# Three pairs of w_conv_out's columns as seven products each, with gate, shift and operand sums on GpSimd

## The chip, the core and the metric

The kernel runs on one core of a Trainium2 chip. It is measured in device microseconds, start to end of one execution. Five engines work from queues of their own: TensorE (PE; its weight loads are listed as PEld), VectorE (DVE), ScalarE (ACT), GpSimd (POOL) and SyncE (SP), which here issues nearly all DMAs. An instruction waits on semaphores for what it needs, and behind it waits everything in its engine's queue.

## The reference, cut to what matters

One layer of a transformer trunk: 128 context tokens and 512 latent ones (640 columns in all), width 1024, float32.

```
ada = silu(c) @ w_ada + b_ada              # six parts: sh1, sc1, g1, sh2, sc2, g2
u   = rms_norm(h) * (1 + sc1) + sh1
z   = u @ w_in                             # q, k, v, b_gate, c_gate, x_in, g_att, g_conv
att  = attention(q, k, v) @ w_att_out
conv = (b_gate * dwconv3(c_gate * x_in)) @ w_conv_out
m   = sigmoid(g_att) * att + sigmoid(g_conv) * conv
h   = h + g1 * rms_norm(m @ w_o)
u   = rms_norm(h) * (1 + sc2) + sh2
h   = h + g2 * rms_norm((silu(g) * val) @ w_down),   [g, val] = dwconv3(u @ w_up)
```

The change lies between the gates and `m`: it touches how `conv`, the gate `g1` and the second half of the shift `sh2` are computed.

## The kernel before, in words

Every float32 product is made of three matmuls: weights and right operand are cut into a high part (ACT rounds it) and a low part (VectorE subtracts), and `mm3` adds high x high, high x low and low x high. The 640 tokens are two halves of 320 (`HT`). A weight tile is 128 x 1024: eight blocks of 128 rows for one tile of 128 output columns (`col_load`, `raw_tile`, three buffers), with `hi_of` (line 1173, ACT) and `lo_of` (line 1177, VectorE) for the parts.

*Plain columns.* `plain_gemm` makes one tile of output columns: 8 blocks x 3 matmuls x 2 halves = 48 matmuls of 320 columns.

*Pairs.* `mix(m, extra)` makes two tiles of output columns from seven products where 2 x 2 quarters would take eight: the weights of the two tiles give A11, A12, A22 and four sums S1 to S4 (`msums`, line 1281, four additions of 128 x 512), the right operand gives B11, B21, B22 and the sums T1 to T4. One product is `block`: 4 blocks x 3 matmuls = 12. The seven follow as A11, A12, S2, S1, S3, S4, A22, with ACT's and VectorE's work written between them; S2 and S1 use the weight sums s1, s2 (part 1), S3 and S4 use s3, s4 (part 2), S2 uses T2, S1 T1, S3 T3, A22 T4, S4 B22. Three PSUM banks take the products; ACT copies one (`copied`) and VectorE adds the other (`added`, line 1197). `extra` holds work of other kinds by slot: slot 0 is ahead of A11, slot 1 ahead of A12, 2 ahead of S2, 3 ahead of S1, 4 ahead of S3, 5 ahead of S4, 6 ahead of A22.

*The order of the stages around the change.* After attention and the eight columns of `w_att_out` come 19 pairs of `w_in`: three of g_att (GA), then four times C, X and B, which give `c_gate`, `x_in` and `b_gate` for two tiles each, then four of g_conv (GC). With every C, X, B the convolution's taps (`conv_tap`, line 1405) and products run on VectorE, and its result is stored as `BH`, `BL`, the high and low part (`b_hi`, `b_lo`), the right operand of `w_conv_out`. Then come the eight columns of `w_conv_out`, all by `plain_gemm`, each followed on VectorE by the product with sigmoid(g_conv), the sum with `MA` (the attention's part, line 1525), and the two parts `MH`, `ML` for `w_o`. Then `w_o`: first columns 0 to 511 in four quarters of two blocks, for five tiles of tokens, then columns 512 to 1023.

*Gates.* The gates are products of two vectors (silu of c and of c_ctx) with `w_ada`. `gate_add` (line 292) multiplies a 128-row block of `w_ada` by one number per partition and adds it to a sum, on VectorE; `gate_sums` (line 301) adds over the partitions with four matmuls against ones. Before, the second half of `sh2` (columns 512 to 1023, 512 columns wide) runs on VectorE in the pairs 0 to 7, with `gate_sums` ahead of pair 9 and the way through DRAM (`sht`) to columns by pair 12. The whole of `g1` (1024 wide) runs on VectorE in the eight columns of `w_conv_out`, sixteen passes, with `gate_sums` and `gate_rows` in the second quarter of `w_o`; its rows go through DRAM (`bct`) to `WR` in the third quarter.

*What sets the order.* The orders of TensorE, ACT and VectorE are those in which the program writes them (`fixed`). GpSimd's and SP's instructions are put in order by a planner with costs of its own, except in blocks under `manual_schedule` for that engine; the eight columns of `w_conv_out` are such a block for SP. Rooms in SBUF are named (`r0` to `r7b`); a new tile in a room waits for the last use of the old one.

Of the kernel before, what the change touches and what calls it, by code (L numbers as in the profile page):

```python
# [11 lines left out]
F32 = mybir.dt.float32  # L12
F32R = mybir.dt.float32r
# [4 lines left out]
D = 1024  # L18
# [45 lines left out]
def trunk_layer(ctx, tc, x_prompt, x_sample, cache_k, cache_v, c, c_ctx, w_ada, b_ada, g_pre1, g_post1, g_pre2,  # L64
# [209 lines left out]

    def gate_load(raw, kind, k, c0=0):
        nc.sync.dma_start(raw, w_ada[k * 128:(k + 1) * 128, kind * D + c0:(kind + 1) * D])

# [976 lines left out]
    PAIRS = [("GA", i) for i in range(1, 4)] + [(x, i) for i in range(4) for x in "CXB"] + [("GC", i) for i in range(4)]  # L1254
    NP = len(PAIRS)
    AT = {"GA": O_GA, "C": O_C, "X": O_X, "B": O_B, "GC": O_GC}
    ROWS_OF = {"C": 0, "X": 1, "B": 2}

    def mrows(m):
        x, i = PAIRS[m]  # L1260
        r = ROWS_OF[x] if x in ROWS_OF else (i - 1 if x == "GA" else i)
        return ROWS[2 * r], ROWS[2 * r + 1]

    def col_load(key, w, c0):
        raw = raws[key] = raw_tile()
        nc.sync.dma_start(raw.rearrange("p (k c) -> p k c", c=128), w[:, c0:c0 + 128].rearrange("(k p) c -> p k c", p=128))

    def mload(n):

        if n < 2 * NP:  # L1270
            x, i = PAIRS[n // 2]
            col_load(("m", n // 2, n % 2), w_in, AT[x] + (2 * i + n % 2) * 128)
        elif n < 2 * NP + KT:
            col_load(("v", n - 2 * NP), w_conv_out, (n - 2 * NP) * 128)

    def msums(m):
        a1, a2 = raws["m", m, 0], raws["m", m, 1]
        s1, s2, s3, s4 = (MS[:, i * 512:(i + 1) * 512] for i in range(4))

        def add(out, a, b):  # L1280
            V.tensor_tensor(out=out, in0=a, in1=b, op=ALU.add)  # L1281

        def both():
            add(s1, a2[:, 0:512], a2[:, 512:1024])
            add(s3, a1[:, 0:512], a2[:, 0:512])
        return both, lambda: add(s2, s1, a1[:, 0:512]), lambda: add(s4, s2, a1[:, 512:1024])

    def mhi(m, part):
        src = {0: raws["m", m, 0], 1: MS[:, 0:1024], 2: MS[:, 1024:2048], 3: raws["m", m, 1][:, 512:1024]}[part]
        hi_of(("m", m, part), src)  # L1290
# [5 lines left out]
    def mix(m, extra):  # L1296

        d0, d1 = mrows(m)
        nxt = m + 1 if m + 1 < NP else None
        pair["m", m] = tuple(bank((3 * m + i) % 8)[:, 0:HT] for i in range(3))  # L1300

        def step(x):
            b = 1 if x == "A12" else 2 if x in ("S1", "S4") else 0
            part, half = PLACE[x]
            block(pair["m", m][b], ("m", m, part), half, "m" + RIGHT[x], x in ("A11", "A12", "S1"), True)

# [3 lines left out]

        if m:
            mix_last(m - 1)
# [27 lines left out]
        lo_of(("m", m, 3))  # L1340
        mload(2 * m + 4)
        if nxt:
            mhi(nxt, 0)
            lo_of(("m", nxt, 0))
            adds[1]()
        else:
            vcut(0)
# [6 lines left out]
        if nxt:  # L1354
            adds[2]()
        mload(2 * m + 5)
        more(6)
# [61 lines left out]
    SHIFTS = {(0, 4): ((0, 0), (0, 1)), (1, 1): ((1, 0), (1, 1)), (2, 1): ((2, 0), (2, 1)), (3, 1): ((3, 0), (3, 1)), (4, 1): ((4, 0), (4, 1)),  # L1419
              (4, 4): ((5, 0), (5, 1)), (7, 1): ((6, 0),), (7, 4): ((6, 1), (7, 0), (7, 1))}  # L1420

    def shift_rows():
        p = bank(7)[:, 0:256]
        gate_sums(p, xaccs)
        out = XG[:, 2, 0:256]
        S.activation(out, p, AF.Copy)
        for h in range(2):
            for row in range(2):
                j, r0 = 64 * h + 32 * row, 4 * row + 2 * h
                nc.sync.dma_start(sht[r0:r0 + 2, :].rearrange("(o f) c -> o (f c)", o=1), out[j:j + 1, :])  # L1430
        shr = sm_.tile([KT, 128], F32, name="shr", bufs=1)
        nc.sync.dma_start(shr, sht)
        return shr

# [5 lines left out]

    for k in range(3):
        gate_load(XG[:, 2 + k, :], 3, k, 512)
    for m, (x, i) in enumerate(PAIRS):
        ex = {}
        if m == 9:
            shr = shift_rows()
        elif m == 12:
            shift_columns(shr, bank(7))

# [21 lines left out]
        elif before[0] == "B":  # L1471
# [7 lines left out]
            also(3, b_lo, o, y1)  # L1479
        for slot in (1, 4):  # L1480
            for k, row in SHIFTS.get((m, slot), ()):
                also(slot, gate_add, xaccs, XG[:, 2 + k % 3, :], k, row)
                if row and k + 3 < KT:
                    also(slot, gate_load, XG[:, 2 + k % 3, :], 3, k + 3, 512)
        mix(m, ex)


    MH = [region(rb, f"r5{x}", [4, NTOK], F32R, f"MH{x}") for x in "ab"]
    ML = [region(rb, f"r6{x}", [4, NTOK], F32R, f"ML{x}") for x in "ab"]
    units += [(w_o, 2 * q, 2, 0, 512) for q in range(4)]  # L1490
# [4 lines left out]

    GA0, GA1 = (region(ra, f"r{i}", [5, D], F32, f"GA{i}") for i in range(2))
    gaccs, gvec = [[GA0[:, i, :]] for i in range(2)], GA0[:, 4, :].rearrange("p (i c) -> p i c", i=2)
    graws = [GA1[:, k, :] for k in range(5)] + [GA0[:, k, :] for k in (2, 3)] + [GA1[:, 0, :]]


    loads = ctx.enter_context(ExitStack())
    loads.enter_context(tc.manual_schedule(engines={mybir.EngineType.SP}))
    for j in range(KT):
        if j + 1 < KT:
            vcut(j + 1)
        else:
# [12 lines left out]
        outs = plain_gemm(j + 2, hi, lo, BH, BL)
        sg = ROWS[j]  # L1520
        for h, (out, (b0, b1)) in enumerate(zip(outs, BLKS)):
            times(sg[:, b0:b1], out, sg[:, b0:b1])
            if h == 0 and j:
                gate_add(gaccs, graws[j], j, 0)
        V.tensor_tensor(out=sg, in0=sg, in1=MA[:, j, :], op=ALU.add)
        for row in range(0 if j == 0 else 1, 2):
            gate_add(gaccs, graws[j], j, row)
        mh, ml = MH[j // 4][:, j % 4, :], ML[j // 4][:, j % 4, :]
        S.activation(mh, sg, AF.Copy)
        minus(ml, sg, mh.bitcast(F32))  # L1530

# [388 lines left out]
    for q in range(4):  # L1920
# [7 lines left out]
        elif q == 1:  # L1928
            half_load(0)
            p = bank(6)  # L1930
            gate_sums(p, gaccs)
            gate_rows(p, gvec, GA0[:, 3, 0:512], 0)
            half_cut(0)
# [331 lines left out]
```

## Time and profile before

| | |
|---|---|
| median of 3 runs | 1111.45 us (1111.35 to 1111.68) |
| the profiled execution | 1111.6 us |
| its span, first to last instruction | 1109.7 us |
| granted TensorE clock, mean | 0.999 |
| the 19 pairs of w_in, from the first product | 321.5 to 555.6 us |
| the eight columns of w_conv_out | 555.6 to about 611.9 us |
| GpSimd busy in these two stretches | 0.0 us |

A row of a group gives the line, engine, operation, output <- inputs by the program's names, shapes and count, then after the bar the summed time in us and the mean in ns, then the idle time ahead of these instructions and what ended it. Rows of the timeline have the start and the length in us. The tile `MT` stands for T1 to T4, `UH`, `UL` for the parts of u, `whi`, `wlo` for the parts of a weight tile, `WA`, `WB` for the rows of results and the weight sums, `b` for a PSUM bank of this stage; `s` for one in the attention stage.

### The profile page before, as it was taken

What the parts mean: (1) busy time and instruction counts of PE and PEld (TensorE: products, weight loads), DVE (VectorE), ACT (ScalarE), POOL (GpSimd) and SP (SyncE); (2) the same over time, 40 slices, a digit from 0 to 9 for tenths busy, and PEclk for the clock granted to TensorE, in tenths of its full rate; (3) what the DMA queues carried; (4) which work ended last, traced back from release to release, by engine and by line L of the source; (5) the groups of instructions that cost most, each with busy time, mean ns of one, the idle gap of its engine ahead of it and who ended that gap; (6) DMA issues with size and microseconds to landing.
All of it is one profiled execution on the core that took longest, in us unless ns stands there. A gap on an engine that the chain in (4) does not pass through costs nothing.

```text
span 1109.7 us, 19293 instructions
## 1 busy us (share of the span) xinstructions
PE 1100.2 (99%) x7665; PEld 1014.8 (91%) x7665; DVE 840.1 (76%) x1351; ACT 577.3 (52%) x1021; POOL 146.2 (13%) x190
## 2 busy tenths in 40 slices
PE   8999999999999999999999999999999999999997
PEld 6798888889999999999999789999999999998886
DVE  5687766765548899888678558898899989989544
ACT  5486776664335544455422356655565555546442
POOL 1066566651000000000000022000000000000001
PEclk9999999999999999999999999999999999999999
DMA  9833112102224322332264644234344333435722
GB/s 321 241 100 99 58 40 77 39 2 77 66 89 118 109 76 78 98 93 76 80 207 151 212 170 152 76 100 125 113 130 134 106 114 119 127 100 186 260 91 95
DMA packets 160527, 130.59 MB, mean 118 GB/s; under 512 B 6454, under 2 KB 139054, under 8 KB 160438
## 3 DMA queue, kind: packets, MB, share of 16 engines
q1 hardware_dynamic: 160326, 129.34, 37.4%
q8 instruction: 60, 0.98, 0.4%
q14 instruction: 29, 0.24, 0.1%
q10 hardware_dynamic: 112, 0.04, 0.0%
HBM read 117.91 MB, written 11.44 MB: 117 GB/s over the span
## 4 chain that ended last, share of the span: by engine, by line
PE 96%; DMA 2%; ACT 1%; DVE 1%; POOL 0%; issue 0%; DVEq 0%; SPq 0%; ACTq 0%; POOLq 0%
PE b L1186 45%; PE b L183 10%; PE b L185 9%; PE b L184 9%; PE s L704 3%; PE s L892 3%; PE s L183 3%; PE s L916 3%; PE s L185 3%; PE s L184 3%; DMA raw<-in_w_in_dram 1%; DMA araw<-in_w_ada_dram 1%; PE b L1784 1%; PE s L675 0%; PE s L238 0%; PE b L1634 0%
## 5 line engine op out<-in xcount | busy, mean ns | idle before, releaser
L1186 PE MATMUL b<-ZBr,whi 128*128 128x320 f32 x688 | 152.1, 309 | 0.0
L1186 PE MATMUL b<-MT,whi 128*128 128x320 f32 x608 | 134.2, 309 | 0.0
L1186 PEld LDWEIGHTS b<-ZBr,whi 128*128 128x128 f32 x688 | 114.9, 188 | 0.1
L1186 PE MATMUL b<-ZBr,wlo 128*128 128x320 f32 x344 | 106.1, 308 | 0.0
L1186 PEld LDWEIGHTS b<-MT,whi 128*128 128x128 f32 x608 | 101.6, 188 | 0.0
L1186 PE MATMUL b<-MT,wlo 128*128 128x320 f32 x304 | 94.0, 309 | 0.0
L879 POOL TENSOR_TENSOR pr<-pr,sm 128x640 f32<-128x640 f32 x64 | 80.0, 1260 | 54.6 <-DVE sm L878 48.3
L1173 ACT ACTIVATE whi<-SUM 128x1024 fp32r<-128x1024 f32 x40 | 42.2, 1054 | 78.5 <-DVE SUM L1699 76.0
L1729 DVE SCALAR_TENSOR_TENSOR Y<-C,cffn,Y 128x642 f32<-128x642 f32 x88 | 77.6, 881 | 0.9
L149 DVE TENSOR_TENSOR wlo<-raw,whi 128x1024 fp32r<-128x1024 f32 (+1 forms) x32 | 35.4, 1106 | 53.7 <-ACT whi L148 53.4
L869 ACT ACTIVATE pr<-s,mx,rq 128x640 f32<-128x640 f32 x64 | 56.6, 885 | 32.5 <-DVE mx L856 29.1
L1186 PE MATMUL b<-ZBT,whi 128*128 128x320 f32 x320 | 71.1, 309 | 0.0
L1186 PE MATMUL b<-UL,whi 128*128 128x320 f32 x228 | 70.8, 311 | 0.0
L1186 PE MATMUL b<-UH,wlo 128*128 128x320 f32 x228 | 70.0, 307 | 0.0
L1186 PE MATMUL b<-UH,whi 128*128 128x320 f32 x228 | 69.7, 306 | 0.0
L1173 ACT ACTIVATE whi<-WB 128x1024 fp32r<-128x1024 f32 x38 | 40.1, 1055 | 54.9 <-DVE WB L1281 54.9
L1177 DVE TENSOR_TENSOR wlo<-raw,whi 128x1024 fp32r<-128x1024 f32 (+1 forms) x51 | 50.4, 1018 | 21.7 <-ACT whi L1173 21.6
L1186 PEld LDWEIGHTS b<-ZBr,wlo 128*128 128x128 f32 x344 | 64.6, 188 | 0.0
L183 PE MATMUL s<-whi,UH 128*128 128x256 f32 (+1 forms) x197 | 64.4, 327 | 0.0
L1194 ACT ACTIVATE p<-b 128x320 f32<-128x320 f32 x78 | 34.2, 438 | 56.7 <-PE b L1186 54.8
L851 DVE TENSOR_REDUCE mx<-s 128x1 f32<-128x640 f32 x64 | 52.5, 820 | 14.6 <-PE s L704 14.2
L185 PE MATMUL s<-whi,UL 128*128 128x256 f32 (+1 forms) x197 | 59.8, 304 | 0.0
(401 smaller groups left out, 3191.5 us busy)
## 6 DMA issues: line engine op xcount, KB each, us to landing
raw<-in_w_in_dram SPq DMA_DIRECT2D x48, 512.0 KB, 3.8
RAW<-in_w_up_dram SPq DMA_DIRECT2D x40, 512.0 KB, 5.0
raw<-in_w_down_dram SPq DMA_DIRECT2D x22, 512.0 KB, 5.0
raw<-in_w_ada_dram SPq DMA_DIRECT2D x18, 512.0 KB, 5.1
actd<-Y SPq DMA_DIRECT2D x18, 321.0 KB
XT<-in_w_ada_dram SPq DMA_DIRECT2D x9, 512.0 KB, 9.7
raw<-in_w_conv_out_dram SPq DMA_DIRECT2D x9, 512.0 KB, 3.8
raw<-in_w_att_out_dram SPq DMA_DIRECT2D x8, 512.0 KB, 3.9
```

What stands on the lines that cost most here:

```text
L149: V.tensor_tensor(out=lo[:, :n], in0=raw, in1=hi[:, :n].bitcast(F32), op=ALU.subtract)
L183: PE.matmul(out, ah, bh, start=start, stop=False)
L184: PE.matmul(out, ah, bl, start=False, stop=False)
L185: PE.matmul(out, al, bh, start=False, stop=stop)
L851: V.tensor_reduce(out=mx, in_=self.sc[h], axis=AX.X, op=ALU.max, negate=True)
L869: S.activation(pr, self.sc[h], AF.Exp, bias=mx, scale=rs, accum_out=sm)
L879: G.tensor_tensor(out=pr, in0=pr, in1=sm.broadcast_to((128, NTOK)), op=ALU.mult)
L1173: S.activation(to[0], raw, AF.Copy)
L1177: V.tensor_tensor(out=lo, in0=raw, in1=hi.bitcast(F32), op=ALU.subtract)
L1186: PE.matmul(out, p[:, ws], q[:, k, :], start=start and k == 0 and n == 0, stop=stop and k == 3 and n == 2, skip_group_check=True)
L1194: S.activation(t, pair[j][b], AF.Copy)
L1729: V.scalar_tensor_tensor(out=y, in0=crows(j)[i][:, d:d + NACT], scalar=cffn[:, 44 * d + o:44 * d + o + 1], in1=y, op0=ALU.mult, op1=ALU.add)
```

## The change

- **w_conv_out.** Columns 0 and 1 stay plain. Columns 2 to 7 become three pairs (`PAIRS += [("O", 1..3)]`, `mix` with m = 19, 20, 21). Their right operands are quarters of `BH`, `BL` and four sums oT1 to oT4, kept in the room of u's parts. oT1 (B12 - B11) is built during the w_in pairs: the difference on GpSimd (`first_sum`, four of 128 x 320), the parts on ACT and VectorE (`first_hi`, `first_lo`). The others come from Q2, Q3, Q4: eight operations of 128 x 1280 on GpSimd in the rooms of the old T1 and T3, written behind the last GC pair, with parts on ACT and VectorE (`last_parts`).
- **Weight sums of these pairs.** `msums` runs on GpSimd for m >= 19, on VectorE as before for the others.
- **Gating.** `gated` multiplies by sigmoid(g_conv) on VectorE and adds `MA` on GpSimd (VectorE for the last pair); `out_hi`, `out_lo` make `MH`, `ML`.
- **Gate and shift.** `g1` in two halves and the half of `sh2` are three streams of eight blocks of 128 x 512, by `sum_add` on GpSimd: for each of two rows a `tensor_scalar` into a temporary and a `tensor_tensor` that adds it to the sum (the first block only the `tensor_scalar`). Two rooms take the blocks by turns; the load of the block after next is issued behind each `sum_add`. `ADDS` places them in the slots of the pairs 0 to 10, and `sum_done` (with `gate_sums`, 256 columns) in (3, 4), (7, 0) and (10, 4). All of this leaves the column stage and `w_o`.
- **Order.** From the last GC pair to the end of the new pairs GpSimd's order is the written one too.

```diff
+    PAIRS += [("O", i) for i in range(1, 4)]
+    LAST = len(PAIRS) - 1
...
     def mload(n):
-        if n < 2 * NP:
+        j = n - 2 * NP
+        if j < 0:
             x, i = PAIRS[n // 2]
             col_load(("m", n // 2, n % 2), w_in, AT[x] + (2 * i + n % 2) * 128)
-        elif n < 2 * NP + KT:
-            col_load(("v", n - 2 * NP), w_conv_out, (n - 2 * NP) * 128)
+        elif j < KT:
+            col_load(("v", j) if j < 2 else ("m", n // 2 - 1, n % 2), w_conv_out, j * 128)
+        elif j < KT + 3:
+            fetch(state["next"] + j - KT + 1)
...
         def add(out, a, b):
-            V.tensor_tensor(out=out, in0=a, in1=b, op=ALU.add)
+            (V if m < NP else G).tensor_tensor(out=out, in0=a, in1=b, op=ALU.add)
...
-    def shift_rows():
...
+    SUMMED = ((2, 0), (2, 512), (3, 512))
+    stream = [(c, k) for c in range(3) for k in (*range(KT), *(("vec",) if c < 2 else ()))]
+    def sum_room(c, k):
+        return XG[:, 3 + stream.index((c, k)) % 2, :]
...
+    def sum_add(c, k):
+        raw, tm = sum_room(c, k), XG[:, 2, :]
+        for row in range(2):
+            x, a = s32[:, 32 * k + 30 + row:32 * k + 31 + row], XG[:, row, :]
+            G.tensor_scalar(out=tm if k else a, in0=raw, scalar1=x, scalar2=None, op0=ALU.mult)
+            if k:
+                G.tensor_tensor(out=a, in0=a, in1=tm, op=ALU.add)
+        sum_load()
+
+    def sum_done(c, m):
+        p, out = bank((3 * m + 4) % 8)[:, 0:256], XG[:, 2, 0:256]
         gate_sums(p, xaccs)
...
+    ADDS = {(0, 1): (0, 0), (0, 4): (0, 1), (1, 1): (0, 2), (1, 3): (0, 3), (1, 5): (0, 4), (2, 1): (0, 5), (2, 3): (0, 6), (2, 5): (0, 7),
+            (3, 4): (0, None), (3, 5): (1, 0), (4, 1): (1, 1), (4, 3): (1, 2), (4, 5): (1, 3), (5, 1): (1, 4), (5, 3): (1, 5), (5, 5): (1, 6),
+            (6, 1): (1, 7), (7, 0): (1, None), (7, 1): (2, 0), (7, 4): (2, 1), (8, 1): (2, 2), (8, 3): (2, 3), (8, 5): (2, 4), (9, 1): (2, 5),
+            (9, 5): (2, 6), (10, 1): (2, 7), (10, 4): (2, None)}
...
+    def first_sum(out, y):
+        G.tensor_tensor(out=out[:, :HT], in0=y[:, :HT], in1=y[:, HT:], op=ALU.subtract)
...
+    loads.enter_context(tc.manual_schedule(engines={mybir.EngineType.SP, mybir.EngineType.Pool}))
...
+    gadd(Q3, h12, l12)
+    gadd(Q3, h22, Q3, ALU.subtract)
+    gadd(Q3, Q3, l22)
+    gadd(Q2, t1h, t1l)
+    gadd(Q2, Q2, h22)
+    gadd(Q2, Q2, l22)
...
+    for j in range(2):
+        first = NP
+        if j == 0:
+            vcut(1)
+        else:
+            hi_of(("m", first, 0), raws["m", first, 0])
+            lo_of(("m", first, 0))
+            adds = msums(first)
+            for f in adds:
+                f()
+            gadd(Q4, Q2, h21, ALU.subtract)
+            gadd(Q4, Q4, l21, ALU.subtract)
+        mload(2 * NP + 4 + j)
         _, hi, lo = cut["v", j]
         outs = plain_gemm(j + 2, hi, lo, BH, BL)
+        if j == 0:
+            last_parts("T3", Q3)
+        else:
+            last_parts("T2", Q2, -1.0)
+            mhi(first, 1)
+        for out, (b0, b1) in zip(outs, BLKS):
+            times(ROWS[j][:, b0:b1], out, ROWS[j][:, b0:b1])
+        V.tensor_tensor(out=ROWS[j], in0=ROWS[j], in1=MA[:, j, :], op=ALU.add)
+
+    def gated(m, i, eng):
+        j, d = 2 * PAIRS[m][1] + i, mrows(m)[i]
+        times(ROWS[j], d, ROWS[j])
+        eng.tensor_tensor(out=ROWS[j], in0=MA[:, j, :], in1=ROWS[j], op=(ALU.add, ALU.subtract)[i])
+
+    for m in range(NP, LAST + 1):
+        j = 2 * PAIRS[m - 1][1] if m > NP else 0
+        ex = {i: [] for i in range(7)}
+        if m == NP:
+            ex[4].append(lambda: last_parts("T4", Q4))
+        else:
+            ex[1] += [lambda i=i: gated(m - 1, i, G) for i in range(2)]
+        for i in range(2):
+            ex[6 if m == NP else 4 + i] += [lambda i=i: out_hi(j + i), lambda i=i: out_lo(j + i)]
+        mix(m, ex)
```

More of the change, by code (lines that the diff above doesn't have):

```diff
@@ L1304, in step @@
             part, half = PLACE[x]
-            block(pair["m", m][b], ("m", m, part), half, "m" + RIGHT[x], x in ("A11", "A12", "S1"), True)
+            block(pair["m", m][b], ("m", m, part), half, ("m" if m < NP else "o") + RIGHT[x], x in ("A11", "A12", "S1"), True)
         def more(i):
@@ L1435, in shift_columns @@
+        if c < 2:
+            sum_load()
+        else:
+            late["shift"] = sm_.tile([KT, 128], F32, name="shr", bufs=1)
+            nc.sync.dma_start(late["shift"], sht)
     def shift_columns(shr, p):
@@ L1518, in trunk_layer @@
         _, hi, lo = cut["v", j]
         outs = plain_gemm(j + 2, hi, lo, BH, BL)
[L1520 to L1528, printed above, removed]
```

154 lines of the change are left out of this document (98 added, 56 removed).

## The prediction

> **What bounds the kernel now.** I read the page first, for the shares of the engines.
>
> ```profile
> span 1109.7 us, 19293 instructions
> ...
> PE 1100.2 (99%) x7665; PEld 1014.8 (91%) x7665; DVE 840.1 (76%) x1351; ACT 577.3 (52%) x1021; POOL 146.2 (13%) x190
> ```
>
> TensorE is busy for the whole span but 9.5 us, so a removed matmul is worth its full interval as long as nothing makes TensorE wait. The profiled execution took 1111.6 us around this span, 0.15 above the median of the runs, 1111.45; I add the sum to the median. The chain that ended last, asked for the stretch from the first seven-product pair to the first column of w_conv_out and then for the w_o stage, gives the intervals (start, length, what):
>
> ```profile
> 321.50 110.36 PE b L1186 x756
> 431.86 0.57 PE b L301 x8
> 432.43 36.99 PE b L1186 x252
> 469.42 0.15 PE b L1436
> 469.58 86.00 PE b L1186 x588
> ...
> 618.83 1.00 PE b L301 x8
> ```
>
> 756 matmuls in 110.36 us are 0.146 us each, back to back. One product is 12 of them, 1.75 us; one pair is 84, 12.3 us. L301 is `gate_sums`: 0.57 us with 256 columns, 1.00 us with 512. The busy times by stretch cover twelve pairs (321.4 to 469.4) and the eight plain columns of w_conv_out:
>
> ```profile
> 321.40:469.40 148.00, 148.00 (x1018) 147.19 (x1016) 127.63 (x189) 72.11 (x113) 0.00 (x0) 1.00 0.32 95
> 555.60:611.90 56.30, 56.30 (x385) 56.30 (x385) 43.59 (x52) 14.46 (x18) 0.00 (x0) 1.00 0.56 179
> ```
>
> The columns are length, PE, weight load, DVE, ACT, POOL. TensorE has no hole in either stretch, a plain column is 56.3 / 8 = 7.04 us, VectorE is busy for 127.63 of 148 us among the pairs, and GpSimd is idle. The change fills that idle GpSimd, so the question is what GpSimd's work costs, and whether it costs VectorE anything.
>
> **Removed.** Three pairs of 84 matmuls stand in place of six columns of 48: 36 x 0.146 = 5.26 us less on TensorE. `gate_sums` at 512 columns goes (1.00) and there are three at 256 in place of one: +2 x 0.57 - 1.00 = +0.14. The sixteen `gate_add` passes on VectorE in the column stage and the sixteen among the pairs go too. As TensorE waits nowhere there, that alone gains nothing; it frees port time, counted below.
>
> **What GpSimd gets.** These are its large groups, and the smallest one:
>
> ```profile
> L879 POOL TENSOR_TENSOR pr<-pr,sm 128x640 f32<-128x640 f32 x64 | 80.0, 1260 | 54.6 <-DVE sm L878 48.3 <-PE s L892 3.3 <-ACT PT L897 2.8
> ...
> L640 POOL TENSOR_TENSOR qf<-qf,zt 128x256 f32<-128x256 f32 x13 | 9.5, 730 | 3.3 <-PE s L704 2.2 <-DVE qf L639 1.0
> ...
> L651 POOL TENSOR_SCALAR ssq<-ssq 128x4 f32<-128x4 f32 x25 | 4.8, 193 | 3.4 <-DVE ssq L650 1.4
> ...
> L875 POOL TENSOR_TENSOR pr<-pr,smc 128x512 f32<-128x512 f32 x4 | 4.2, 1040 | 7.6 <-DVE smc L874 7.6
> ```
>
> L879 and L875 multiply by a broadcast scalar; L640 has two full operands, as the new adds have. From 193 ns (4 elements) to 730 ns (256) the slope is 2.13 ns an element, so a two-operand add takes by estimate 1.275 us at 512, 2.91 us at 1280, 1.55 us at 640, 0.87 us at 320. The lower bound, the slope of L875, gives 1.04, 2.3, 1.26 and 0.72. `tensor_scalar` with 512 elements is not in the trace: it lies between 0.19 and 1.04 us. It streams one operand for the add's two, so I take half the slope: 0.73 us.
>
> One stream (eight `sum_add`) is 16 x 0.73 + 14 x 1.275 = 29.5 us. It has from pair 0 to step S3 of pair 3, 3.57 x 12.3 = 44 us; the next two have 42 and 45. So GpSimd by itself is in time, even with 1.04 us for the `tensor_scalar` (34.5 us). All three streams with the four `first_sum` are 48 x 0.73 + 42 x 1.275 + 4 x 0.87 = 92 us, inside the first 10.57 pairs, 130 us.
>
> **Whether it costs VectorE.** The attention stage has the two engines side by side. I looked in the timeline for moments in which a large GpSimd operation meets a VectorE operation with two inputs in SBUF. There are three:
>
> ```profile
> 82.62 0.67 DVE L817 TENSOR_TENSOR wlo<-raw,whi 128x512 fp32r<-128x512 f32 x1
> ...
> 82.71 1.69 POOL L879 TENSOR_TENSOR pr<-pr,sm 128x640 f32<-128x640 f32 x1 [0.42 <-DVE sm L878]
> ```
>
> ```profile
> 75.54 0.31 DVE L856 TENSOR_TENSOR mx<-mx,rq 128x1 f32<-128x1 f32 x1
> ...
> 74.80 1.04 POOL L875 TENSOR_TENSOR pr<-pr,smc 128x512 f32<-128x512 f32 x1 [3.58 <-DVE smc L874]
> ```
>
> ```profile
> 91.18 0.38 DVE L856 TENSOR_TENSOR mx<-mx,rq 128x1 f32<-128x1 f32 x1
> ...
> 90.29 1.25 POOL L879 TENSOR_TENSOR pr<-pr,sm 128x640 f32<-128x640 f32 x1
> ...
> L856 DVE TENSOR_TENSOR mx<-mx,rq x61: 158/159/378, 75.5 to 252.4; 128x1 f32<-128x1 f32 x61
> ```
>
> In the first, VectorE was there first; GpSimd's 1.25 us operation took 1.69 us and ended 1.11 us after VectorE's did (84.40 against 83.29). In the other two GpSimd was first; a VectorE operation whose median is 159 ns took 0.31 and 0.38 us and ended with GpSimd's (75.85 against 75.84, 91.56 against 91.54). So the second waits until the first is through: they take turns. From the ends, about 0.14 us at the start and 0.15 us at the end of a GpSimd operation do not block. The Trainium skill, page "SBUF — State Buffer", section "SBUF: two separate sides", has the rule: VectorE's second pair of ports is GpSimd's only one, an exclusive lock, and a VectorE instruction with two SBUF inputs fully blocks against a GpSimd one that reads SBUF. The three meetings agree, and the sum without this rule is the first rival below.
>
> Now VectorE's share of the turns. These rows (321.4 to 469.4) are its main work there, what the change takes off (L292, L290) and what has one input in PSUM and doesn't take part (L1197):
>
> ```profile
> L1177 DVE TENSOR_TENSOR wlo<-WB,whi 128x1024 fp32r<-128x1024 f32 x23 | 28.1, 1222 | 4.6 <-ACT whi L1173 4.6
> ...
> L292 DVE SCALAR_TENSOR_TENSOR XG<-XG,s 128x512 f32<-128x512 f32 x14 | 9.8, 745 | 0.0
> ...
> L1177 DVE TENSOR_TENSOR wlo<-raw,whi 128x512 fp32r<-128x512 f32 x12 | 8.2, 682 | 0.0
> L1197 DVE TENSOR_TENSOR WA<-b,p 128x320 f32<-128x320 f32 x16 | 7.8, 490 | 15.6 <-PE b L1186 15.6
> ...
> L1197 DVE TENSOR_TENSOR WB<-b,p 128x320 f32<-128x320 f32 x8 | 3.9, 486 | 0.9 <-PE b L1186 0.9
> L1197 DVE TENSOR_TENSOR WA<-b,u 128x320 f32<-128x320 f32 x8 | 3.9, 482 | 0.0
> ...
> L1365 DVE TENSOR_TENSOR MA<-MA,WA 128x640 f32<-128x640 f32 x4 | 3.1, 817 | 0.0
> L1197 DVE TENSOR_TENSOR WB<-b,u 128x320 f32<-128x320 f32 x4 | 1.9, 482 | 0.0
> ...
> L290 DVE TENSOR_SCALAR XG<-XG,s 128x512 f32<-128x512 f32 x2 | 0.9, 479 | 0.0
> ```
>
> 127.63 - 9.8 - 0.9 - 17.5 = 99.4 us of two-input work in twelve pairs, 8.3 us a pair, 87.5 us in 10.57 pairs, and 1.9 us for the four `first_lo` (0.48 each, as L1197): 89.4 us. The turns need 89.4 + 92.1 = 181.5 us where TensorE gives 130: 51 us too much. If 0.29 us of each of the 94 GpSimd operations doesn't block, GpSimd takes 65 us and the excess is 24 us. I take the middle, **+38 us**, as handing over will cost some of that 0.29. VectorE can't put its work off: the low halves (L1177) are weights of the next product, and `gate_sums` holds TensorE's queue until GpSimd's sums are there. Behind a late GpSimd the SP queue stands too, as a `sum_load` waits for its room and weight loads are behind it; that only moves the same wait.
>
> **Between the last GC pair and the first new pair.** Rows for the new operands (VectorE's and ACT's halves of 1280, ACT's of 1024):
>
> ```profile
> L1237 DVE TENSOR_TENSOR MT<-WA,MT 128x1280 fp32r<-128x1280 f32 x2 | 3.0, 1484 | 0.0
> ...
> L1236 ACT ACTIVATE MT<-WA 128x1280 fp32r<-128x1280 f32 x2 | 2.5, 1271 | 2.1 <-DVE WA L1200 2.1
> ```
>
> ```profile
> L1173 ACT ACTIVATE whi<-raw 128x1024 fp32r<-128x1024 f32 x12 | 12.6, 1051 | 0.0
> ```
>
> GpSimd can start on Q3 when S1 of the last GC pair is through with the room of T1. From there TensorE reaches S2 of the first new pair after three products, two columns and two products: 5.25 + 14.08 + 3.5 = 22.8 us. S2 needs the sums s1 and s2 with their low half. GpSimd: six operations of 1280 (17.5) and three of 512 (3.8) = 21.3, ACT 1.05, VectorE 1.22: 23.6, a wait of 0.8 us even without turns. With turns, VectorE's two-input work in that time comes in between: three low halves of 1024 and one of 512, one `MA` addition, T3's and T2's low halves = 3.7 + 0.7 + 0.8 + 3.0 = 8.1 us. Then S2 starts at 31.7, 8.9 us late.
>
> T4 for A22: s4 and two operations on Q4, 7.1 us after s2, then T4's halves (1.27 + 1.49), the addition after S3 (0.49) and the low half of 512 (0.68), which is behind T4's on VectorE: 3.9. Without turns 21.3 + 7.1 + 3.9 = 32.3, where A22 is due at 30.6: 1.7 us. With turns 29.4 + 7.1 + 3.3 (two low halves and an addition) + 3.9 = 43.7 where A22 is due at 38.7: 5.0 us. So **+13.9 us** with turns (8 with the lower prices and the 0.29 us off, up to 19 if the second pair, with 7.6 + 8.2 us of turns in 12.3, is late too), **+2.5** without. After the last pair, `gated` and the halves of rows 6 and 7 end some 5 us later; w_o asks for them in its fourth quarter, three times 6.9 us on (611.9 to 618.83 is the first). They cost nothing, unless a unit's low half behind them slips past those 6.9 us.
>
> **Sum:** 1111.45 - 5.26 + 0.14 + 38 + 13.9 = 1158.2 us.
>
> **Rivals.** *No turns* (faster or the same): the three meetings are chance, or the rooms of the new operands don't collide. Then all of GpSimd's sums are in time and 1111.45 - 5.12 + 2.5 = 1108.8 us, or 1107.8 at the lower price of the adds, where only A22's 1.5 us are left. It decides from the point where the two engines' turns fit into 130 us, that is if GpSimd blocked for under 40 of its 92 us. For it: GpSimd ends in time by itself. Against it: three meetings out of three. Chance 0.16; since the gain lies at the 2.2 us that a measurement can tell (0.2%), 0.11 of it count as faster and 0.05 as the same.
>
> *Short turns*: GpSimd holds the other off for half of its time only. Then 89.4 + 46 - 130 = 5 us, and some 6 us before the first new pair: 1111.45 - 5.12 + 11 = 1117 us, up to 1135 with three fifths. For it: 0.29 us of each operation are already free, and GpSimd's chain of dependent steps leaves gaps. Against it: L856 waited until the very end both times. Chance 0.09, most of it slower.
>
> *Full turns*: the forecast, 0.75. Its own range: 1111.45 - 5.1 + 24 + 8 = 1138 to 1111.45 - 5.1 + 51 + 19 = 1176.
>
> **Chances and range.** The range reaches from 1122, within the short turns, to 1178; it leaves out the case without turns. Faster 0.11, the same 0.06, slower 0.83.
>
> **What would show it.** In the profile after, with full turns: L1177 with 1024 elements has a mean well over 1222 ns between the first and the eleventh pair and 1222 behind it, GpSimd's `tensor_tensor` of 512 are over 1.275 us, TensorE shows holes behind VectorE's low halves and ahead of `gate_sums`, a pair takes some 16 us instead of 12.3 up to the eleventh and 12.3 in the four GC pairs. S2 and A22 of the first new pair wait for VectorE. If L1177 stays at 1222 ns beside a busy GpSimd, the main step is wrong and the time is under 1110. If the pairs are long while L1177 is not, it is another wait: SP's weight loads behind `sum_load`, or GpSimd's price.

## The result and the profile after

| | before | after |
|---|---|---|
| median, 5 runs each on the same chip | 1111.45 us (1111.27 to 1112.08) | 1191.15 us (1190.91 to 1191.76) |
| ratio after / before, 95% interval | | 1.0717 [1.0701, 1.0732] |
| granted TensorE clock, mean | 0.999 | 0.976 |

The kernel is 79.7 us slower: the sign that was forecast, but 33 us more than the forecast and above its range. The page of after, its span, busy times and two rows of slices (one digit for 29.75 us):

```profile
span 1190.0 us, 19436 instructions
...
PE 1119.8 (94%) x7637; PEld 1021.5 (86%) x7637; DVE 881.1 (74%) x1333; ACT 591.5 (50%) x1046; POOL 382.6 (32%) x308
...
PE   8999999999994957879997899999999999999998
...
PEclk9999999999997998989999999999999999999999
...
PE 69%; POOL 11%; issue 10%; DVE 6%; DMA 2%; ACT 1%; SPq 0%; DVEq 0%; POOLq 0%; ACTq 0%
```

TensorE was idle for 9.5 us of the span before and is now idle for 70. The holes lie in the 13th to the 18th digit (357 to 535 us, pairs of w_in with sums) and, smaller, in the 22nd and 23rd (625 to 684 us, where the new pairs begin). GpSimd, which had no part in the end before, carries 11% of the chain that ended last. The waits of after name two kinds (who <- whom: us in total, times, longest):

```profile
PEld b L301 <- POOL XG L1464: 37.8, 6, 13.2
...
PE b L301 <- POOL XG L1464: 34.3, 6, 12.9
...
PE b L1186 <- DVE wlo L1177: 13.6, 15, 2.3
```

L301 is `gate_sums`: TensorE waits 34.3 us in all for the last addition (L1464) of GpSimd's sums. L1186 are the products, which wait in many small pieces for VectorE's low halves. The new operations on GpSimd, grouped by shape (busy us, mean ns, then idle time):

```profile
L1462 POOL TENSOR_SCALAR XG<-XG,s 128x512 f32<-128x512 f32 x48 | 108.1, 2253 | 79.5 <-DMA XG<-in_w_ada_dram 73.5 <-DVE WA L1197 2.2
...
L1464 POOL TENSOR_TENSOR XG<-XG 128x512 f32<-128x512 f32 x42 | 63.7, 1517 | 3.3
...
L1590 POOL TENSOR_TENSOR Zr5a<-BHa,BL 128x1280 f32<-128x1280 f32 x1 | 3.0, 2960 | 101.9 <-PE b L1186 101.9
```

The sums take 171.8 us of GpSimd where the prediction gave them 48 x 0.73 + 42 x 1.275 = 88.6. The timeline shows both kinds first beside a busy VectorE, then in a hole, where VectorE is idle (start, length):

```profile
344.69 2.94 POOL L1462 TENSOR_SCALAR XG<-XG,s 128x512 f32<-128x512 f32 x1
347.71 1.74 POOL L1464 TENSOR_TENSOR XG<-XG 128x512 f32<-128x512 f32 x1
...
377.40 1.56 POOL L1462 TENSOR_SCALAR XG<-XG,s 128x512 f32<-128x512 f32 x1
379.05 1.26 POOL L1464 TENSOR_TENSOR XG<-XG 128x512 f32<-128x512 f32 x1
380.41 1.56 POOL L1462 TENSOR_SCALAR XG<-XG,s 128x512 f32<-128x512 f32 x1
```

Alone, the two-operand add takes 1.26 us, as estimated (1.275), and the `tensor_scalar`, with one operand, takes 1.56 us, twice its estimate and half as much again as its upper bound. From start to start the two are 3.01 us. VectorE's subtractions beside the sums, from 321 to 520 us:

```profile
L1177 DVE TENSOR_TENSOR wlo<-WB,whi 128x1024 fp32r<-128x1024 f32 x21 | 34.4, 1636 | 4.2 <-ACT whi L1173 4.2
...
L1177 DVE TENSOR_TENSOR wlo<-raw,whi 128x1024 fp32r<-128x1024 f32 x10 | 12.1, 1214 | 0.0
L1177 DVE TENSOR_TENSOR wlo<-raw,whi 128x512 fp32r<-128x512 f32 x10 | 12.1, 1209 | 0.0
```

Two of the three kinds are 1.3 and 1.8 times as long as before (1222 and 682 ns); the third, which stands elsewhere in the order, has its old 1217 ns: what is held depends on what meets. Behind the last sum, from 530 to 580 us, the first row is back at its old length:

```profile
L1177 DVE TENSOR_TENSOR wlo<-WB,whi 128x1024 fp32r<-128x1024 f32 x8 | 9.8, 1223 | 1.4 <-ACT whi L1173 1.2
```

Last, busy times around the first hole, which reaches from 367.4 to 384 us, its part from 372 us on once more by itself (length, PE, weight load, DVE, ACT, POOL, granted clock, DMA):

```profile
333.40:367.40 34.00, 32.65 (x217) 31.51 (x216) 32.23 (x33) 16.98 (x27) 32.55 (x17) 1.00 0.42 121
367.40:384.00 16.60, 1.73 (x9) 0.38 (x8) 2.77 (x4) 1.90 (x3) 15.11 (x10) 0.65 0.15 46
372.00:384.00 12.00, 1.69 (x8) 0.38 (x8) 0.00 (x0) 0.00 (x0) 10.69 (x8) 0.52 0.14 43
384.00:388.00 4.00, 4.00 (x19) 3.62 (x14) 1.10 (x2) 0.00 (x0) 3.11 (x2) 0.50 0.04 9
388.00:392.00 4.00, 4.00 (x24) 4.00 (x24) 3.84 (x6) 1.00 (x1) 2.02 (x1) 0.82 0.78 231
392.00:396.00 4.00, 4.00 (x30) 4.00 (x29) 1.43 (x2) 1.91 (x4) 3.82 (x3) 1.00 0.57 166
```

Three things are to be seen. Ahead of the hole TensorE loses only 1.4 of 34 us in pieces, with VectorE and GpSimd both busy for 95%; in the second and the third stream (396 to 438.5 and 459 to 507.8 us) the pieces are 6.9 and 6.8 us. In the hole TensorE loses 14.9 us in `gate_sums`, and from 372 us on only GpSimd works: VectorE, which has nothing left that does not hang on TensorE, stands too. Behind it TensorE is busy, but the granted clock is 0.50, then 0.82; the two stretches lose 4 x 0.50 + 4 x 0.18 = 2.7 us. Two more holes, which end at 451 and 517 us, have a low clock behind them as well (0.59 and 0.50 in the first 4 us; full behind 4 and 8 us).

### The profile page after: what moved, and what is told of

Its sections match the earlier page's. It is cut to its first block, busy times and chain, and to the rows that moved or that the text cites. A ratio compares the mean times of both kernels' runs of the same rounds, so it can differ in the third digit from the quotient of the medians.

```text
span 1190.0 us, 19436 instructions
## 1 busy us (share of the span) xinstructions
PE 1119.8 (94%) x7637; PEld 1021.5 (86%) x7637; DVE 881.1 (74%) x1333; ACT 591.5 (50%) x1046; POOL 382.6 (32%) x308
## 4 chain that ended last, share of the span: by engine, by line
PE 69%; POOL 11%; issue 10%; DVE 6%; DMA 2%; ACT 1%; SPq 0%; DVEq 0%; POOLq 0%; ACTq 0%
PE b L1186 27%; PE b L185 7%; PE b L184 7%; PE b L183 7%; POOL XG L1462 5%; POOL XG L1464 3%; PE s L704 3%; PE s L892 3%; PE s L183 3%; PE s L916 3%; PE s L185 3%; PE s L184 3%; DVE wlo L1177 2%; POOL Zr5a L1590 2%; DVE WA L1420 1%
## 5 line engine op out<-in xcount | busy, mean ns | idle before, releaser
L1186 PE MATMUL b<-ZBr,whi 128*128 128x320 f32 x688 | 152.1, 309 | 0.0
L1186 PE MATMUL b<-MT,whi 128*128 128x320 f32 x608 | 138.1, 315 | 6.2 <-ACT u L1194 3.6
L1462 POOL TENSOR_SCALAR XG<-XG,s 128x512 f32<-128x512 f32 x48 | 108.1, 2253 | 79.5 <-DMA XG<-in_w_ada_dram 73.5
L1186 PEld LDWEIGHTS b<-ZBr,whi 128*128 128x128 f32 x688 | 114.9, 188 | 0.1
L1186 PEld LDWEIGHTS b<-MT,whi 128*128 128x128 f32 x608 | 103.3, 191 | 9.6 <-issue 4.9
L1186 PE MATMUL b<-ZBr,wlo 128*128 128x320 f32 x344 | 106.1, 308 | 0.0
L1186 PE MATMUL b<-MT,wlo 128*128 128x320 f32 x304 | 97.6, 321 | 8.9 <-DVE wlo L1177 8.8
L1186 PE MATMUL b<-UH,whi 128*128 128x320 f32 x276 | 88.2, 320 | 3.4 <-DVE MD L1197 1.9
L1186 PE MATMUL b<-UH,wlo 128*128 128x320 f32 x276 | 88.2, 320 | 2.2 <-DVE wlo L1177 2.2
L1186 PE MATMUL b<-UL,whi 128*128 128x320 f32 x276 | 88.6, 321 | 0.0
L1177 DVE TENSOR_TENSOR wlo<-raw,whi 128x1024 fp32r<-128x1024 f32 (+1 forms) x51 | 64.7, 1302 | 19.0 <-ACT whi L1173 18.9
L149 DVE TENSOR_TENSOR wlo<-raw,whi 128x1024 fp32r<-128x1024 f32 (+1 forms) x32 | 35.4, 1107 | 52.1 <-ACT whi L148 51.7
L1194 ACT ACTIVATE p<-b 128x320 f32<-128x320 f32 x84 | 36.8, 438 | 69.3 <-PE b L1186 67.5
L1186 PE MATMUL b<-ZBT,whi 128*128 128x320 f32 x320 | 71.1, 309 | 0.0
L1186 PEld LDWEIGHTS b<-MT,wlo 128*128 128x128 f32 x304 | 58.3, 192 | 13.2 <-DVE wlo L1177 12.0
L1464 POOL TENSOR_TENSOR XG<-XG 128x512 f32<-128x512 f32 x42 | 63.7, 1517 | 3.3
```

Of the source, the lines that this page charges most:

```text
L1177: V.tensor_tensor(out=lo, in0=raw, in1=hi.bitcast(F32), op=ALU.subtract)
L1186: PE.matmul(out, p[:, ws], q[:, k, :], start=start and k == 0 and n == 0, stop=stop and k == 3 and n == 2, skip_group_check=True)
L1194: S.activation(t, pair[j][b], AF.Copy)
L1462: G.tensor_scalar(out=tm if k else a, in0=raw, scalar1=x, scalar2=None, op0=ALU.mult)
L1464: G.tensor_tensor(out=a, in0=a, in1=tm, op=ALU.add)
```

## The experiments

The question is how the 79.7 us divide, and by which mechanism. The theory: GpSimd's sums are late because `tensor_scalar` is dear, and the two engines hold each other off. Rivals: GpSimd is late merely by its own length; another wait (SP's queue behind `sum_load`); only one of the two operations holds VectorE off. All kernels are edits of after. Each is one run unless its count is given, told as the difference from the kernel before on the same chip, which lay between 1111.26 and 1112.24 us; differences under 1 us are not read. The edits concern these lines of `sum_add`, called SUM below:

```python
            G.tensor_scalar(out=tm if k else a, in0=raw, scalar1=x, scalar2=None, op0=ALU.mult)
            if k:
                G.tensor_tensor(out=a, in0=a, in1=tm, op=ALU.add)
```

**e1, the late part alone.** SUM becomes the product of the first block only.

```diff
-            G.tensor_scalar(out=tm if k else a, in0=raw, ...)
-            if k:
-                G.tensor_tensor(out=a, in0=a, in1=tm, op=ALU.add)
+            if k == 0:
+                G.tensor_scalar(out=a, in0=raw, scalar1=x, scalar2=None, op0=ALU.mult)
```

> The gate's and the shift's sums are left out but for the first block of each stream (6 of 90 GpSimd operations stay, the loads and gate_sums too), so g1 and half of sh2 are wrong. Theory, turns at VectorE's second port: the first eleven pairs lose their wait of some 64 us, the stretch behind the last GC pair keeps its own: 1121 to 1130 us. Rival, the new pairs are what is slow: still over 1170 us.

Measured 1125.99, that is +14.4. With the 5.12 us of matmuls removed, the late part loses 19.5 us, and the sums in the first pairs account for 79.7 - 14.4 = 65.3. The next kernels are read against e1.

**e4, the sums alone.** All eight columns plain, without `first_sum`; the sums as in after.

```diff
-            col_load(("v", j) if j < 2 else ("m", n // 2 - 1, n % 2), w_conv_out, j * 128)
...
+            col_load(("v", j), w_conv_out, j * 128)
...
-            also(3, first_sum, b0, y0)
-            also(3, first_sum, b1, y1)
...
-    loads.enter_context(tc.manual_schedule(engines={mybir.EngineType.SP, mybir.EngineType.Pool}))
+    loads.enter_context(tc.manual_schedule(engines={mybir.EngineType.SP}))
+    for j in range(KT):
```

> The sums on GpSimd as in the change, but all eight columns of w_conv_out plain (no new pairs, no first_sum, nothing on GpSimd behind pair 10). Turns: the first eleven pairs lose 60 to 65 us against the kernel before, and nothing else is lost: 1170 to 1177 us. Rival, the new pairs: 1111 to 1120 us.

Measured 1171.45, +59.9. From both sides, then, the sums cost 60 to 65 us: they are the main loss, and it isn't made by the new pairs of w_conv_out.

**e2, the same length with nothing large read.** The operations become powers of 128x4, which are as long as an addition.

```diff
+            for _ in range((2 - row if k == 0 else 1 if k == KT - 1 else 3)):
+                G.tensor_tensor(out=pw, in0=ones[:, 0:4], in1=mhalf[:, 0:4], op=ALU.pow)
```

> Each tensor_scalar and tensor_tensor of 512 elements is replaced by pow operations of 128x4, about 1.0 us each, so that GpSimd is busy as long as its sums are alone (45 us a stream for 43) but streams nothing from SBUF; only the last block of each stream gets its real tensor_scalar, so g1 and half of sh2 are wrong. Turns: VectorE goes on beside it, and TensorE waits only for the 3 to 6 us by which a stream is longer than its pairs: 1128 to 1145 us. Rival, GpSimd's bare length: 64 us stay, 1180 to 1190 us. Rival, SP's queue with sum_load ahead of weight loads: the same, 1170 to 1190 us.

Measured 1184.45, +72.9: at first sight a blow to the turns. But the control wasn't one. Its row on GpSimd:

```profile
L1467 POOL TENSOR_TENSOR XG<-ones,mhalf 128x4 f32<-128x4 f32 x123 | 149.8, 1218 | 9.3
```

The power, 1.015 us in the attention stage, takes 1.218 here on average (1.006 at least, 2.659 at most): even an operation of four elements waits for VectorE, so the streams got longer than planned. VectorE itself was not held (its subtraction of 1024 stayed at 1222 to 1280 ns), and VectorE's weight sums waited 18.3 us for weights, which stood in SP's queue behind `sum_load`. So e2, which came out where both its rivals were expected, shows that GpSimd's lateness and the SP queue behind it can cost some 58 us over e1 without VectorE being held. It does not part these two.

**e5, the same length with nothing read.** Memsets, which only write, in numbers that make up the length of a stream.

```diff
+            if row == 0:
+                G.tensor_scalar(out=tm[:, 0:4], in0=raw[:, 0:4], scalar1=x, scalar2=None, op0=ALU.mult)
+            for _ in range(5 if k else 3):
+                G.memset(a, 0.125)
```

> Each tensor_scalar and tensor_tensor of 512 is replaced by memsets of 128x512 into the sum (5 for a row step, 3 for the first block; by the trace's 338 ns for 286 elements some 0.55 us each, 42 us a stream), with one tensor_scalar of 4 elements a block that reads the room, so SP and gate_sums wait for GpSimd as in the change. g1 and half of sh2 are wrong. A memset reads nothing. Turns on the read side: VectorE stays at 1222 ns in L1177, GpSimd is in time or a few us late: 1128 to 1142 us. Rival, GpSimd's bare length and the queues that wait for it: 1170 to 1186 us.

Measured 1132.85, +20.6, 6.2 over e1. GpSimd's row and VectorE's:

```profile
L1465 POOL MEMSET XG<- 128x512 f32 x228 | 108.4, 526 | 68.1 <-PE b L185 65.6 <-PE b L301 2.5
L1463 POOL TENSOR_SCALAR XG<-XG,s 128x4 f32<-128x4 f32 x24 | 19.7, 823 | 3.7 <-DMA XG<-in_w_ada_dram 3.5 <-POOL XG L1465 0.2
```

```profile
L1177 DVE TENSOR_TENSOR wlo<-WB,whi 128x1024 fp32r<-128x1024 f32 x30 | 37.3, 1245 | 5.5 <-ACT whi L1173 5.4
```

108.4 + 19.7 = 128.1 us, exactly what the sums would take alone (48 x 1.56 + 42 x 1.27 = 128.2), cost a tenth of what the sums cost. So it is not GpSimd's own length: the sums lose by what GpSimd and VectorE do to each other. With no slack the 6.2 us are there (summed over windows of 2 us from 321 to 530 us, TensorE is idle for 4.7 us and loses 1.5 to the clock), but they are small.

**e6, nobody waits for GpSimd.** Twenty of the 24 blocks are summed from a block that stays in its room, and `gate_sums` reads another room.

```diff
+            src = XG[:, 3, :]
+            if (c, k) < (2, 4):
+                G.tensor_scalar(out=tm if k else a, in0=src, scalar1=x, scalar2=None, op0=ALU.mult)
...
-        gate_sums(p, xaccs)
+        gate_sums(p, [[XG[:, 4, :]]] * 2)
```

> GpSimd runs the first 20 of 24 row blocks (75 operations, 107 us alone) on one block that stays in its room; gate_sums reads another room, so neither TensorE nor SP waits for GpSimd; g1 and half of sh2 are wrong. Turns, part one, VectorE held up: L1177 is long and TensorE waits behind VectorE: 1145 to 1170 us. Rival, only the wait for GpSimd's results counts (gate_sums held 34 us in the change): 1126 to 1133 us, as without sums.

Measured 1150.72, +38.5, 24.1 over e1. VectorE's rows from 321 to 520 us:

```profile
L1177 DVE TENSOR_TENSOR wlo<-WB,whi 128x1024 fp32r<-128x1024 f32 x27 | 39.4, 1458 | 4.3 <-ACT whi L1173 4.0
L1292 DVE TENSOR_TENSOR WB<-WB,raw 128x512 f32<-128x512 f32 x26 | 25.1, 965 | 0.0
```

VectorE is held off (1255 and 683 ns in e1, 1636 and 900 in after, in the same window), and that alone costs 24 us. By difference, the other 41 of the 65 come with the waits for GpSimd; that is a subtraction, as e6 also sums four blocks fewer.

**e12, the products alone.** All 48 `tensor_scalar`, none of the additions.

```diff
-            G.tensor_scalar(out=tm if k else a, in0=raw, scalar1=x, scalar2=None, op0=ALU.mult)
-            if k:
-                G.tensor_tensor(out=a, in0=a, in1=tm, op=ALU.add)
+            G.tensor_scalar(out=tm if 0 < k < KT - 1 else a, in0=raw, scalar1=x, scalar2=None, op0=ALU.mult)
```

> GpSimd keeps the 48 tensor_scalar of 512 elements (1.56 us alone, 25 us a stream of 44) and loses the 42 additions; the last block's product goes into the sum in place of all, so g1 and half of sh2 are wrong. If a tensor_scalar holds VectorE off for its length as an addition does (e8 over e9 paid 32 us for 36 additions of 1.27 us, 0.7 of their time), 48 x 1.56 x 0.7 = 52 us, or by port time alone 89 + 75 + 3 for 130, 37 us: 1150 to 1178 us. Rival, the long tensor_scalar reads only for a part of its time: 1128 to 1145 us.

Measured 1135.95, +24.5, 10.1 over e1. GpSimd's row, then VectorE's from 321 to 520 us:

```profile
L1462 POOL TENSOR_SCALAR XG<-XG,s 128x512 f32<-128x512 f32 x48 | 106.9, 2232 | 90.4 <-DMA XG<-in_w_ada_dram 80.0 <-PE b L301 7.5
```

```profile
L1177 DVE TENSOR_TENSOR wlo<-WB,whi 128x1024 fp32r<-128x1024 f32 x29 | 36.2, 1249 | 5.3 <-ACT whi L1173 5.2
L1292 DVE TENSOR_TENSOR WB<-WB,raw 128x512 f32<-128x512 f32 x30 | 21.0, 700 | 0.0
```

The expected 1150 to 1178 us missed; the time is in the rival's range. The hold is one-sided. The `tensor_scalar` waits for VectorE (2232 ns against 1561 alone), while VectorE goes at its own pace (1249 and 700 ns). So what lengthened VectorE's rows in after and e6 were the two-input additions; e8, next, has them without the products.

**e8 and e9, the products on ScalarE.** In e8 ScalarE makes the 48 products and GpSimd only adds; e9 leaves out the additions but the last block's.

```diff
-            G.tensor_scalar(out=tm if k else a, in0=raw, scalar1=x, scalar2=None, op0=ALU.mult)
+            pr = a if not k else raw if row else tm
+            S.activation(pr, raw, AF.Copy, scale=x)
             if k:
-                G.tensor_tensor(out=a, in0=a, in1=tm, op=ALU.add)
+                G.tensor_tensor(out=a, in0=a, in1=pr, op=ALU.add)
```

> The 48 tensor_scalar go to ACT (about 0.63 us each), GpSimd keeps the 42 additions of 512 (1.27 us alone, 18 us a stream of 44). Result as the reference. Turns: 42 x 1.27 + 89 + 3 = 146 us of port time for 130, 12 us less without the free ends: 1130 to 1145 us. Rival, only GpSimd's lateness counts: it is 20 us early in each stream, 1126 us.

> As e8, but of GpSimd's 42 additions only the six of the last blocks stay; ACT's 48 products stay in their places, so g1 and half of sh2 are wrong. It parts e8's two suspects. GpSimd's additions in VectorE's way: near the kernel without sums, 1126 to 1136 us. Rival, ACT's products stand in ACT's queue ahead of the high halves (e8's chain shows them): 1155 to 1167 us.

e8 measured 1167.03 (+54.8), e9 1134.94 (+23.7, 9.3 over e1). e8 missed, and e9 shows by what: 36 additions that take 36 x 1.27 = 45.7 us on GpSimd cost TensorE 54.8 - 23.7 = 31.1 us. VectorE in e8:

```profile
345.84 1.75 DVE L1292 TENSOR_TENSOR WB<-raw 128x512 f32<-128x512 f32 x1
347.50 1.74 DVE L1292 TENSOR_TENSOR WB<-raw,raw 128x512 f32<-128x512 f32 x1
```

Each of these two additions of weights, 0.68 us in e9, lasts through one of GpSimd's; on average the two kinds take 1.22 us, the other additions of weights keep 0.68. They stand ahead of the low halves that the next product waits for, so little of it is hidden: from 321 to 530 us TensorE is idle for 26.2 us and loses 9.9 to the clock, 5.4 and nothing in e9, which is the whole difference. `gate_sums` doesn't wait for GpSimd in e8, so it isn't late sums that cost this. The waits are for VectorE's additions of the products (15.6 us) and low halves (5.8); part of it may run through ACT's queue, where VectorE waits 6.0 us for ACT's products, 3.0 in e9. The expectation came from a balance of the port's time against the pairs' time (16 us too much); such a balance misses in which order the operations meet.

**e10, the product as a two-operand operation.** The `tensor_scalar` becomes a `tensor_tensor` with the scalar broadcast.

```diff
-            G.tensor_scalar(out=tm if k else a, in0=raw, scalar1=x, scalar2=None, op0=ALU.mult)
+            G.tensor_tensor(out=tm if k else a, in0=raw, in1=x.broadcast_to((128, 512)), op=ALU.mult)
```

> The 48 tensor_scalar on GpSimd (1.56 us alone) become tensor_tensor with the number broadcast, the form that took 1.04 us in the attention stage. Result as the reference. If GpSimd's length is what is paid (port time, and the time by which a stream is late), 48 x 0.52 = 25 us of GpSimd go: 1164 to 1178 us. Rival, each meeting costs the same whatever its length, or TensorE waits for something else: 1184 to 1191 us.

Measured 1182.68, +71.4, 8.3 better than after. The product's lengths (minimum, median, maximum):

```profile
L1462 POOL TENSOR_TENSOR XG<-XG,s x48: 1042/1372/2025, 324.9 to 502.0; 128x512 f32<-128x512 f32 x48
```

48 x 0.52 = 25 us less of GpSimd alone bring 8 us: the shorter form is a two-input one, and now holds VectorE. The time is in neither expected range. From 321 to 520 us VectorE's subtractions are longer than in after (1636 and 1214 ns):

```profile
L1177 DVE TENSOR_TENSOR wlo<-WB,whi 128x1024 fp32r<-128x1024 f32 x22 | 37.5, 1706 | 2.1 <-ACT whi L1173 2.1
...
L1177 DVE TENSOR_TENSOR wlo<-raw,whi 128x1024 fp32r<-128x1024 f32 x11 | 21.5, 1959 | 0.0
```

The loss moves from TensorE's wait for GpSimd (34.3 us in after, none here) to its wait for VectorE (for the low halves 20.7 us, 8.8 in after, from 318 to 530 us).

**e3, e7, e13: the work on VectorE.** e3 makes the sums on VectorE (as before the change, 0.75 us a block and row). e7 is e1 with the new pairs' operands, weight sums and gating on VectorE, part of it some slots earlier or later. e13 is both.

```diff
-            G.tensor_scalar(out=tm if k else a, in0=raw, ...)      # e3, e13
+            gate_add(xaccs, raw, k, row)
...
-            (V if m < NP else G).tensor_tensor(out=out, in0=a, in1=b, op=ALU.add)      # e7, e13
+            V.tensor_tensor(out=out, in0=a, in1=b, op=ALU.add)
...
-        G.tensor_tensor(out=out, in0=a, in1=b, op=op)
+        V.tensor_tensor(out=out, in0=a, in1=b, op=op)
```

> The 48 row steps run on VectorE as one scalar_tensor_tensor each (0.68 us by start to start), in the same slots. Turns: VectorE needs 89 + 33 us of two-input work and 14 us with PSUM in the 130 us of the first 10.6 pairs, a few us too much: 1125 to 1138 us, all but 5 to 10 us of what leaving the sums out gives. Rival, that VectorE's own load is what makes the pairs long: 33 us more on it make it no better than 1175 us.

> No sums as in e1 (g1 and half of sh2 wrong), and behind the last GC pair everything of GpSimd's on VectorE: Q2 to Q4 (1.4 us each), the weight sums, the additions of MA; column 1's product and the MA additions stand a few slots later, T4's parts one slot earlier. Turns: the 36 matmuls come out as time, less 1 to 4 us of waits for T4 and s1: 1107 to 1112 us, against 1126. Rival, the chain of ACT and VectorE there is too long whoever adds: 1118 to 1126 us.

> Only first_sum is left on GpSimd: sums on VectorE as in e3, everything behind the last GC pair on VectorE as in e7. Result as the reference. If the two parts add, 1140.9 - 12.3 = 1128.6 us, 1126 to 1132. Rival, e3's loss was in its late part too and goes with it: under 1116 us.

e3 measured 1140.88 (+29.3, 14.9 over e1), 3 us above what was expected: VectorE does in 15 us of lost time what costs 65 on GpSimd. e7 measured 1113.71 (+1.5), 1.7 us above what was expected: taking the late work from GpSimd, with the moved slots, saves 14.4 - 1.5 = 12.9 us, and 1.5 + 5.1 = 6.6 stay, as VectorE is then full in the last columns. Its windows of e7 (VectorE is the third number behind the length):

```profile
570.00:580.00 10.00, 9.68 (x67) 9.42 (x65) 9.97 (x11) 4.21 (x6) 0.00 (x0) 1.00 0.18 54
580.00:590.00 10.00, 9.26 (x60) 8.80 (x60) 10.00 (x16) 5.32 (x10) 0.00 (x0) 1.00 0.18 53
590.00:600.00 10.00, 7.82 (x51) 7.29 (x51) 9.93 (x14) 4.04 (x7) 0.00 (x0) 1.00 0.18 54
```

e13, four runs, measured 1129.38 (1127.48 to 1130.04), 1.0154 [1.0137, 1.0171] of before. It is 62 us better than after and still slower than before. Even e7, which does no sums at all, isn't under the time before, so none of these experiments points to a version that beats it.

## Why the prediction was right in sign and wrong in size

**The failed step** is the price of `tensor_scalar`: "it lies between 0.19 and 1.04 us. It streams one operand for the add's two, so I take half the slope: 0.73 us". It takes 1.56 us alone. The number of operands was no guide to the price, and a bound from other operations (193 ns for the same operation on four elements, 1.04 for another one of 512) was no bound. Of the 33 us that the forecast was short, 27.3 lie in the first pairs (65.3 in place of 38), where this price counts, and 5.6 in the late part (19.5 in place of 13.9). Two things hung on the price. "GpSimd by itself is in time" fell: by the starts in the timeline a stream alone is 14 x 3.01 + 2 x 1.65 = 45.4 us, where it has 44, 42 and 45, ahead of any turn. And the sum of the turns was short: with 1.56 the prediction's own balance is 89.4 + 48 x 1.56 + 42 x 1.27 + 3.5 - 130 = 91 us, or 64 with 94 x 0.29 us of free ends, in place of 51 and 24; the middle, which the prediction took, would be 78 in place of 38. Measured are 65.3 (e1); the last `gate_sums` starts at about 517 us instead of 321 + 130, which is 66 late.

**The turns** were there, in one direction as predicted and in the other only in part. Each kind of reading operation that GpSimd ran here waits for VectorE's two-input work (1.56 to 2.25 us, 1.015 to 1.218 for four elements), but only GpSimd's two-input ones on large tiles hold VectorE (e12 against e6 and e8). The Trainium skill, page "SBUF — State Buffer", section "SBUF: two separate sides", lets a two-input VectorE instruction block fully against any GpSimd one that reads SBUF; e12's 1249 ns beside 107 us of `tensor_scalar` does not agree. So 64 is near 65 partly by luck, since that balance charges VectorE for operations that did not hold it. e10 is nearer to the prediction's own picture, with 90 operations that are all two-input ones: its balance with 1.04 us gives 66 or 39, and 71.4 - 14.4 = 57.0 are measured. e8, with additions alone, shows that the balance can also be far off (16 against 31.1).

**Where the 65 us lie.** I cut 321 to 525 us of after into windows of 2 us. TensorE is idle for 49.4 us of them: 34.3 in `gate_sums`, the other 15 in pieces, 8.8 of them for VectorE's low halves. Its busy time times one less the granted clock, summed, is 10.8 us. That makes 60.2 of 65.3; the rest isn't assigned. e1, cut in the same way, has 0.5 us idle and nothing lost to the clock, so this is all the sums' doing. The forecast named both kinds of hole; the clock behind them was no step of it, and it is a sixth of the loss (in e2 and e10, cut from 321 to 530 us, 16.0 of 58.5 and 15.0 of 57.0). In e6 the same count gives 13.1 us idle and 6.6 by the clock: even many small holes lower it. The parts do not add by operation: products alone cost 10.1, additions alone 31.1, together 65.3. My reading is that one of the two still fits into a stream's three and a half pairs and both do not; no run varied the slack by itself, so that is argued and not shown.

**The SP queue** ("only moves the same wait") is borne out in after: VectorE's weight sums wait 0.9 us for loads. In e2 VectorE waited 18.3 us for weights behind the same queue, so it can count.

**The late part** was given 13.9 us and lost 19.5. Its first term was nearly right. The chain that ended last in after:

```profile
618.87 2.96 POOL Zr5a L1590
621.91 3.28 POOL Zr5a L1590
625.26 6.77 POOL Zr5a L1590 x2
632.09 3.82 POOL Zr5a L1590
635.98 4.08 POOL Zr5a L1590
640.06 6.54 POOL MS L1292 x3
646.62 1.07 ACT whi L1173
647.71 1.78 DVE wlo L1177
649.53 8.40 PE b L1186 x37
```

The first matmul of S2 that needs the low half starts 649.53 - 618.87 = 30.7 us behind GpSimd's first operation, where 31.7 was forecast. Uncounted was the clock, again (columns as above):

```profile
640.00:650.00 10.00, 5.20 (x31) 4.42 (x30) 9.53 (x9) 3.71 (x4) 9.92 (x6) 0.94 0.05 14
650.00:660.00 10.00, 9.29 (x46) 9.04 (x45) 5.39 (x3) 3.50 (x5) 9.92 (x5) 0.72 0.13 40
660.00:670.00 10.00, 8.79 (x48) 8.56 (x49) 9.75 (x12) 4.15 (x6) 5.02 (x4) 0.83 0.36 105
```

In windows of 2 us from 600 to 720, TensorE is idle for 11.2 us, less than the 13.9 forecast, and loses 4.8 by the clock (e1, from which the 19.5 come, has 9.8 and 6.3 from 540 to 720); some 3.4 of the 19.5 stay unassigned. e7 shows that the work would have stayed late on VectorE as well, by 6.6 us.

**The removed matmuls** and `gate_sums` need no correction: nothing in the runs speaks against 5.12 us, though no run shows them by themselves. The rival without turns is refuted by L1177 (1636 ns where it asked for 1222) and by e8. The short turns (1117 to 1135) missed the time, but they had the wrong price too: with 1.56 us their sum at three fifths is 89.4 + 0.6 x 131.7 - 130 = 38 us, which makes 1159 with the late part as forecast. As a mechanism they are not refuted for every operation, since one kind of GpSimd's held VectorE off for no time that shows.

## What to carry to other kernels

An engine that is idle has no price until the operation that it is to do, in its shape, stands in a trace: measure that first, alone and beside the engine it shares a port with, and take no estimate from the count of operands. Sums on GpSimd that TensorE waits for at a fixed slot need slack for the waits they meet (here 171.8 us of operations that are 128.2 alone); without it each late sum is a hole, and the low clock behind the holes was a sixth of the loss here. VectorE's two-input work that stands ahead of the next weights is a bad neighbour for GpSimd's two-input work: 36 additions of 1.27 us cost 31 us.

## What the runs showed of the hardware

- On GpSimd, 128x512 in fp32: `tensor_scalar` with a scalar of one element per partition 1.56 us, `tensor_tensor` with two full operands 1.26, with a broadcast operand 1.04, memset 0.526. Of the three that read, the one with the fewest tensors to read is the dearest.
- Beside VectorE's two-input work the `tensor_scalar` took 2.23 us on average and left VectorE at its own pace (1249 and 700 ns, 1255 and 683 with no sums); a two-input addition of 128x512 stretched VectorE's additions of 0.68 us to 1.78 us at most (e8).
- A power of 128x4 went from 1.015 to 1.218 us beside VectorE without holding it; memsets kept 526 ns and held nobody.
- Behind the holes of 14.9, 11.4 and 8.1 us in `gate_sums` the granted clock was 0.50, 0.59 and 0.50 in the first 4 us and full after 8 at most. The Trainium skill, page "TensorE: Matmul & The Clock Gate", Part 1, has the clock at half rate after an idle window; the 0.50 agrees. A stretch with several small holes (640 to 650 us, 4.8 us idle) was followed by 0.72.
